# A hybrid decoder trunk: the state space branch with features on partitions

## The chip, the cores and the metric

One core of a Trainium2 chip runs the whole program. The metric is the device time of one execution in microseconds (us); the time of a kernel is the median of its runs, and a profiled execution of each kernel gives the rows shown here.

## What is computed

Two decoder layers over 512 tokens of width 1024, batch 1, all in float32. Each layer projects the normalised input once, feeds three branches (a Mamba-2 state space branch, multi-head latent attention, a gated DeltaNet), projects each branch back to the model width, merges them with gates, and adds a feed-forward part. The change lies in the state space branch. Per group g (two groups, eight heads of 64 features each) and per chunk of 128 tokens:

```python
y_diag = jnp.einsum('bclgn,bcsgn->bcgls', Cc, Bc) * L ...   # decay matrix L, per head
y_off  = jnp.einsum('bclgn,bcgepn,bgecl->bclgep', Cc, h_prev, jnp.exp(A_cum))
...
y = y + d_skip.astype(jnp.float32).reshape(G, E)[:, :, None] * xs
y = y.reshape(Bsz, S, SSD_INNER) * jax.nn.silu(z.astype(jnp.float32))
y = rmsnorm(y.reshape(Bsz, S, G, SSD_INNER // G), norm_g.reshape(G, SSD_INNER // G))
```

(The first line is shortened: the diagonal part multiplies the masked score matrix of a chunk, `CB * L`, with the head's `X = xs * dt`.) The norm runs over the 512 features of a group, for each token.

## The kernel before

**Dense products.** Every weight product is done in three parts (`mm3`, L182 to L184): the operands are split into a rounded part and a remainder, and TensorE multiplies high by high, low by high and high by low. Weights come as 512 KB tiles `wraw` through SyncE's DMA queue (`weights_raw`, L161, two buffers), ScalarE rounds them into `whi` (L154), VectorE forms the remainder `wlo` (L155), four buffers of each. `dense_F` puts features on partitions and streams the 512 tokens; `dense_T` puts tokens on partitions and streams 512 features. The activations are also kept as such pairs: `split_act` (L250, L251) and `split_gain` (L254, L255) make them.

**Order.** The engines run their lists in order. The lists are made at build time by a scheduler that keeps to data dependencies and to buffers of a tile pool (a tag has a number of buffers, and a new tile waits until the old one of that buffer has had its last reader), and that otherwise follows the program's order with some priorities. All loads and stores go through SyncE's one queue (SP), in its order. PSUM has four banks `acc` for dense products, three `sm` and one `yt` for the rest.

**The state space branch** (`ssd_group`, called for g = 0 and 1 in each layer). B and C of the group come with features on partitions (`bt`, `ctl`). The group's 512 features of x come from `dense_F` as well, go through the convolution (`conv_silu`), and are transposed on TensorE (L720) into `xs`, tokens on partitions, by ScalarE's copy (L721). z comes from `dense_T` (`silu_T`), tokens on partitions. Then a loop over the four chunks t:

- the decay matrix of eight heads (two tiles `eE` of four): a broadcast load from `d_c` in DRAM (L448), ScalarE's L450 and L451; B and C's product (L733), masked on VectorE (L735) and multiplied into `eE` (L737);
- `xd = xs * dt` (L739), the eight products of y (L742; stationary side the 128x128 decayed scores, moving side 64 features), the skip term (L744) and its addition to PSUM (L745);
- for t > 0 the contribution of the state (L748; one product, 512 columns moving), scaled by the decay (L750, a factor per row) and added (L751);
- for t < 3 the new state (L754, L756, L759 to L762);
- the gate (L764) and ScalarE's square with a running sum per row (L766).

After the loop the norm's factors come from `rsq` (L258 on VectorE, then a power on GpSimd, L259), scale the rows (L770), and sixteen transposes per block (L775) bring y to features on partitions, where `split_gain` makes the pair `yh`, `yl`. These carry the same tile names as the attention branch's output, so all but the first wait until its last products have read that.

**Around it.** Program order in a layer: front, attention branch, group 0, `gdn_decays` (decay tiles of the later branch, through `eE`, written to `d_e`, L800), half of the attention's output projection, group 1, the other half, `gdn_matrix`, `gdn_blocks` (a chain of 31 steps on VectorE, L857 and L858, and a way through DRAM), then the state space branch's output projection and the two units of the DeltaNet. The DeltaNet's triangular inverse has nine further steps of small products (`first`, L891; `second`, L907 and L908; `last_doubling`, L927 and L929). They are put between the rows of dense products:

```python
        def between():
            if next(rows) >= 23 and steps:
                steps.pop(0)()

        out_proj(a["w_ssd_out"][ly], 0, *ys, br, after=between)
```

`after` is called once per pair of weight tiles, 12 dense products; the output projection has 32 such calls.

Of the kernel before, what the change touches and what calls it, by code (L numbers as in the profile page):

```python
# [20 lines left out]
P = 128  # L21
S = 512
# [12 lines left out]
ROWS = ('ssd_dt_bias', 'gdn_dt_bias', 'ssd_a_log', 'gdn_a_log', 'ssd_d')  # L35
# [20 lines left out]
def hybrid_kernel(ctx, tc, a, out, depth=2, taps=None):  # L56
# [42 lines left out]
    ct = mk(cst, [P, NBLK * P + 104], F32, "ct")  # L99
# [195 lines left out]
    def load_params(ly, rows=True):  # L295
        pc = mk(sp, [P, 155], F32, "pc", 2)
        sync.dma_start(pc, a["pcols"][ly])
        prow = mk(sp, [P, 64], F32, "prow", 2)
        if rows:
            load_rows(prow, ly)  # L300
        return pc, prow
# [49 lines left out]
    for ly in range(depth):  # L351
# [5 lines left out]
        sconv_b, g_n1, g_ssd, g_q, g_kv, g_gdn, g_n2 = 0, 12, 20, 28, 32, 34, 35  # L357
# [32 lines left out]
        d_c = mk(dr, [T, 24 * P], F32, "d_c", 2)  # L390

        def step_sizes():
# [35 lines left out]
            sync.dma_start(d_c.rearrange("t (n l) -> (t n) l", l=P), rows)  # L428
            dec = mk(sp, [P, 3, T, 24], F32, "dec")
# [8 lines left out]
            dsk = mk(sp, [P, 16], F32, "dsk")  # L438
            dve.tensor_scalar(dsk, prow[:, 48:64], 0.25, None, ALU.mult)
# [257 lines left out]
        def ssd_group(g, yh, yl):  # L697
            h0 = 8 * g
            xs = mk(br, [P, T, 512], F32, "tok", 4)
            z = mk(br, [P, T, 512], F32, "tok", 4)  # L700
# [13 lines left out]
            for cp in range(2):  # L714
                for j, pj in enumerate(dense_F(weights(w_in, O_XBC + 512 * g + 256 * cp, 256, D), tiles(256), D, xh, xl)):
                    xf = mk(br, [P, S], F32, "ft4", 2)
                    conv(pj, 4 * g + 2 * cp + j, xf)
                    ps = sm_bank()
                    for t in range(T):
                        pe.transpose(ps[:, t * P : (t + 1) * P], xf[:, t * P : (t + 1) * P], ident)  # L720
# [4 lines left out]
            ss = mk(sp, [P, T], F32, "sss")  # L725
            st = None
            for t in range(T):
# [10 lines left out]
                xd = mk(br, [P, 512], F32, "wk0")  # L738
                dve.tensor_tensor(hv8(xd), hv8(xs[:, t, :]), bc_last(dtq[:, t, h0 : h0 + 8], 64), ALU.mult)  # L739
                py = sm_bank()  # L740
                for h in range(8):
                    pe.matmul(py[:, h * 64 : (h + 1) * 64], e2[h // 4][:, h % 4, :], xd[:, h * 64 : (h + 1) * 64], start=True, stop=True)  # L742
                y = mk(br, [P, 512], F32, "wk1")
                dve.tensor_tensor(hv8(y), hv8(xs[:, t, :]), bc_last(dsk[:, h0 : h0 + 8], 64), ALU.mult)  # L744
# [559 lines left out]
```

## Time and profile before

| | |
|---|---|
| median of 3 runs | 2329.44 us (2326.19 to 2331.61) |
| the profiled execution | 2331.74 us, of which its span 2329.9 us |
| mean granted TensorE clock | 0.993 |
| instructions in the span | 32047 |
| DMA moved | 239.85 MB, mean 103 GB/s |

The span runs from the first to the last instruction of the program; the rest of the execution's time lies around it. In a row of the order of time stand start, duration, engine, line, operation, output<-inputs, shapes and count; in brackets the idle time before it and what ended it. An ordinary float product leaves two records, one for each pass. The durations of TensorE's products overlap.

### The profile page before, as it was taken

To read this page: it belongs to the slowest core of one execution; us is meant where nothing else is said; L and a number is where in the kernel's file an instruction comes from. 1 tells how busy PE (TensorE), PEld (TensorE's weight loads), DVE (VectorE), ACT (ScalarE), POOL (GpSimd) and SP (SyncE) were. 2 spreads that over 40 slices of the span, in tenths; PEclk is the share of its full clock that TensorE was granted. 3 is DMA by queue.
4 is the path that set the end of the run, shared out by engine and by line. 5 is a ranking of instruction groups with operands and counts; after the bars stand their busy time and mean duration, and the time that the engine had idled before them with its cause. 6 is when DMAs were issued, how large, how long until landed. Compare 5 with 4: busy or idle time off the path is not lost.

```text
span 2329.9 us, 32047 instructions
## 1 busy us (share of the span) xinstructions
PE 2295.1 (99%) x11814; PEld 1891.3 (81%) x11814; DVE 1586.6 (68%) x3116; ACT 1177.7 (51%) x2455; POOL 59.2 (3%) x74
## 2 busy tenths in 40 slices
PE   9999999999999999999999999999999999999998
PEld 8888788878887888888888887888788878888886
DVE  7776666775665458767867765668656645677668
ACT  6766744333443345554657666443334434545545
POOL 0000000000000000000000000000000000000000
PEclk9999999999999999999999999999999999999999
DMA  4223533442222443233132236334422224333231
GB/s 141 78 73 91 172 100 109 123 131 82 78 78 72 145 145 109 75 116 118 50 98 78 78 94 178 91 102 143 111 84 84 67 82 154 127 118 100 91 109 46
DMA packets 208702, 239.85 MB, mean 103 GB/s; under 512 B 33888, under 2 KB 157472, under 8 KB 208544
## 3 DMA queue, kind: packets, MB, share of 16 engines
q1 hardware_dynamic: 208544, 237.80, 33.5%
q8 instruction: 93, 1.52, 0.3%
q14 instruction: 65, 0.53, 0.1%
HBM read 221.41 MB, written 11.63 MB: 100 GB/s over the span
## 4 chain that ended last, share of the span: by engine, by line
PE 89%; DVE 6%; DMA 2%; ACT 2%; POOL 1%; issue 1%; SPq 0%; DVEq 0%; POOLq 0%; ACTq 0%
PE acc L182 23%; PE acc L183 23%; PE acc L184 23%; PE sm L184 2%; PE sm L183 2%; PE sm L182 2%; DVE wlo L155 1%; PE sm L742 1%; DVE tok L858 1%; PE sm L645 1%; DVE gQ L857 1%; PE sm L1015 1%; POOL gms L259 1%; ACT whi L154 1%; PE yt L661 1%
## 5 line engine op out<-in xcount | busy, mean ns | idle before, releaser
L155 DVE TENSOR_TENSOR wlo<-wraw,whi 128x512 fp32r<-128x512 f32 (+1 forms) x552 | 377.4, 687 | 420.3 <-ACT whi L154 402.5
L154 ACT CAST whi<-wraw 128x512 fp32r<-128x512 f32 (+1 forms) x552 | 340.4, 618 | 592.7 <-PE acc L183 379.6
L184 PE MATMUL acc<-xh,wlo 128*128 128x512 f32 (+1 forms) x1248 | 487.3, 391 | 0.0
L182 PE MATMUL acc<-xh,whi 128*128 128x512 f32 (+1 forms) x1248 | 487.2, 391 | 0.0
L183 PE MATMUL acc<-xl,whi 128*128 128x512 f32 (+1 forms) x1248 | 486.3, 390 | 0.0
L183 PEld LDWEIGHTS acc<-xl,whi 128*128 128x128 f32 x1248 | 236.4, 189 | 44.3 <-DVE xl L255 0.4
L184 PEld LDWEIGHTS acc<-xh,wlo 128*128 128x128 f32 x1248 | 236.2, 189 | 44.5
L182 PEld LDWEIGHTS acc<-xh,whi 128*128 128x128 f32 x1248 | 235.9, 189 | 44.3 <-ACT xh L254 0.4
L182 PE MATMUL acc<-yh,whi 128*128 128x512 f32 x384 | 151.9, 399 | 0.0
L183 PE MATMUL acc<-yl,whi 128*128 128x512 f32 x384 | 151.3, 394 | 0.0
L184 PE MATMUL acc<-yh,wlo 128*128 128x512 f32 x384 | 151.3, 394 | 0.0
L686 DVE SCALAR_TENSOR_TENSOR ckl<-acc,pc,ckl 128x511 f32<-128x511 f32 (+2 forms) x168 | 120.3, 744 | 15.5 <-ACT ckl L682 8.2
L154 ACT CAST whi<-wr 128x512 fp32r<-128x512 f32 x128 | 79.5, 621 | 66.6 <-PE acc L184 25.9
L183 PE MATMUL acc<-wlo,xh 128*128 128x512 f32 (+1 forms) x288 | 111.2, 386 | 0.0
L184 PE MATMUL acc<-whi,xl 128*128 128x512 f32 (+1 forms) x288 | 111.0, 387 | 0.0
L182 PE MATMUL acc<-whi,xh 128*128 128x512 f32 (+1 forms) x288 | 109.6, 384 | 0.0
L182 PE MATMUL acc<-whi,yh 128*128 128x512 f32 x256 | 99.7, 389 | 0.0
L184 PE MATMUL acc<-whi,yl 128*128 128x512 f32 x256 | 99.7, 389 | 0.0
L183 PE MATMUL acc<-wlo,yh 128*128 128x512 f32 x256 | 99.6, 389 | 0.0
L155 DVE TENSOR_TENSOR wlo<-wr,whi 128x512 fp32r<-128x512 f32 x128 | 86.1, 687 | 12.1 <-ACT whi L154 11.4
L182 PEld LDWEIGHTS acc<-yh,whi 128*128 128x128 f32 x384 | 71.7, 188 | 16.7 <-ACT yh L254 1.7
L183 PEld LDWEIGHTS acc<-yl,whi 128*128 128x128 f32 x384 | 72.2, 188 | 15.2 <-issue 1.0
(418 smaller groups left out, 4532.1 us busy)
## 6 DMA issues: line engine op xcount, KB each, us to landing
wraw<-in_w_in_dram SPq DMA_DIRECT2D x144, 512.0 KB, 3.6
wraw<-in_w_up_dram SPq DMA_DIRECT2D x64, 512.0 KB, 3.6
wr<-in_w_down_dram SPq DMA_DIRECT2D x32, 1024.0 KB, 5.1
eE<-d_c SPq DMA_DIRECT2D x48, 256.0 KB, 4.0
wraw<-in_w_mla_out_dram SPq DMA_DIRECT2D x16, 512.0 KB, 3.3
eE<-d_e SPq DMA_DIRECT2D x32, 256.0 KB, 3.1
wraw<-in_w_ssd_out_dram SPq DMA_DIRECT2D x16, 512.0 KB, 3.4
wraw<-in_w_gdn_out_dram SPq DMA_DIRECT2D x16, 512.0 KB, 3.3
```

What stands on the lines that cost most here:

```text
L154: act.copy(hi, raw)
L155: dve.tensor_tensor(lo, raw, f32(hi), ALU.subtract)
L182: pe.matmul(o, ah, bh, start=start, stop=False, skip_group_check=more)
L183: pe.matmul(o, ah, bl, start=False, stop=False, skip_group_check=more)
L184: pe.matmul(o, al, bh, start=False, stop=stop, skip_group_check=more)
L259: pool.tensor_tensor(o, o, (exp if exp is not None else nhalf)[:, : o.shape[1]], ALU.pow)
L645: pe.transpose(ps[:, n : n + P], pn[t][:, kb * P : (kb + 1) * P], ident)
L661: pe.matmul(o, v_h, th[:, c : c + w], start=kb == 0, stop=False)
L686: dve.scalar_tensor_tensor(acc[:, d:], ps[:, : S - d], taps_[3 - d], acc[:, d:], ALU.mult, ALU.add)
L742: pe.matmul(py[:, h * 64 : (h + 1) * 64], e2[h // 4][:, h % 4, :], xd[:, h * 64 : (h + 1) * 64], start=True, stop=True)
L857: dve.tensor_tensor(pd, bc_last(nb[:, m, m + 1 :], m + 1), bc_mid(xb[:, m, : m + 1], 31 - m), ALU.mult)
L858: dve.tensor_tensor(xb[:, m + 1 :, : m + 1], xb[:, m + 1 :, : m + 1], pd, ALU.add)
```

## The change

In the state space branch y, z and the norm stand with features on partitions throughout.

- x is kept as it comes (`xf`, features on partitions) and scaled by the skip factor, a column of `pc` now, on ScalarE; VectorE multiplies the transposed x by dt straight out of PSUM (`xd`, for all chunks at once).
- z comes from `dense_F`.
- The products of y change operands: the stationary side is `xd` (64 columns), the moving side the 128 columns of the decayed scores. Even heads write PSUM partitions 0 to 63, odd heads 64 to 127.
- The state's contribution is four products with the state as stationary side; its decay is a factor per token, which stands along the free axis now. A new copy of the exponential of the cumulated decay is written to DRAM (`d_p`) and loaded as broadcast tiles `eb`, two DMAs per chunk.
- The norm's sum of squares: ScalarE squares, VectorE adds four feature tiles to one (two instructions), a product with a column of ones sums over the partitions (in the bank `yt`). The factors are transposed (one product per block), copied, written to DRAM (`d_r`) and loaded again as a broadcast tile `rb`, the same row for all partitions.
- y is multiplied by gain and `rb` in one VectorE instruction per feature tile and split; L775's transposes are gone. The pairs are allocated one by one.
- The tag `tok` has five buffers instead of four.
- The inverse's steps start at the 24th call of `between`, and the last of them falls into the first rows of the DeltaNet's first unit.

The core of the diff:

```diff
+            prows = mk(ml, [96, P], F32, "crowe")
+            act.activation(prows, pc_[:96, :P], AF.Exp)
+            sync.dma_start(d_p.rearrange("t (n l) -> (t n) l", l=P), prows)
...
-                    act.copy(xs[:, :, (2 * cp + j) * P : (2 * cp + j + 1) * P], ps.rearrange("p (t n) -> p t n", t=T))
-            silu_T(br, O_SZ + 512 * g, z)
+                    dve.tensor_tensor(th(xd[:, :, c * P : (c + 1) * P]), th(ps.rearrange("p (t n) -> p t n", t=T)),
+                                      bc_last(dtq[:, :, h0 + 2 * c : h0 + 2 * c + 2], 64), ALU.mult)
+                    act.activation(xf[:, c, :], xf[:, c, :], AF.Copy, scale=dsk[:, 4 * g + c : 4 * g + c + 1])
+            for cp in range(2):
+                for j, pj in enumerate(dense_F(weights(w_in, O_SZ + 512 * g + 256 * cp, 256, D), tiles(256), D, xh, xl)):
+                    silu2(z[:, 2 * cp + j, :], pj)
...
+            pss = y_bank()
...
-                xd = mk(br, [P, 512], F32, "wk0")
-                dve.tensor_tensor(hv8(xd), hv8(xs[:, t, :]), bc_last(dtq[:, t, h0 : h0 + 8], 64), ALU.mult)
                 py = sm_bank()
-                for h in range(8):
-                    pe.matmul(py[:, h * 64 : (h + 1) * 64], e2[h // 4][:, h % 4, :], xd[:, h * 64 : (h + 1) * 64], start=True, stop=True)
-                y = mk(br, [P, 512], F32, "wk1")
-                dve.tensor_tensor(hv8(y), hv8(xs[:, t, :]), bc_last(dsk[:, h0 : h0 + 8], 64), ALU.mult)
-                dve.tensor_tensor(y, y, py, ALU.add)
+                for c in range(4):
+                    for i in range(2):
+                        h = 2 * c + i
+                        pe.matmul(py[64 * i : 64 * i + 64, c * P : (c + 1) * P], xd[:, t, h * 64 : (h + 1) * 64], e2[h // 4][:, h % 4, :], start=True, stop=True)
+                y = xf[:, :, tok]
+                dve.tensor_tensor(y, y, c4(py), ALU.add)
                 if t > 0:
+                    eb = mk(br, [P, 4, P], F32, f"wk{t % 2}")
+                    for i in range(2):
+                        sync.dma_start(eb[64 * i : 64 * i + 64], d_p.rearrange("t (n l) -> t n l", l=P)[t, h0 + i : h0 + 8 : 2].partition_broadcast(64))
                     po = sm_bank()
-                    pe.matmul(po, ctl[:, tok], st, start=True, stop=True)
-                    y2 = mk(br, [P, 512], F32, "wk2")
-                    dve.tensor_tensor(hv8(y2), hv8(po), bc_last(dec[:, 0, t, h0 : h0 + 8], 64), ALU.mult)
-                    dve.tensor_tensor(y, y, y2, ALU.add)
+                    for c in range(4):
+                        pe.matmul(po[:, c * P : (c + 1) * P], st[:, c * P : (c + 1) * P], ctl[:, tok], start=True, stop=True)
+                    dve.tensor_tensor(eb, c4(po), eb, ALU.mult)
+                    dve.tensor_tensor(y, y, eb, ALU.add)
...
-                dve.tensor_tensor(z[:, t, :], z[:, t, :], y, ALU.mult)
-                jk = mk(br, [P, 512], F32, "wk2")
-                act.activation(jk, z[:, t, :], AF.Square, accum_out=ss[:, t : t + 1])
+                zt = z[:, :, tok]
+                dve.tensor_tensor(zt, zt, y, ALU.mult)
+                sq = mk(br, [P, 4, P], F32, "wk2")
+                act.activation(sq, zt, AF.Square)
+                dve.tensor_tensor(sq[:, 0:2], sq[:, 0:2], sq[:, 2:4], ALU.add)
+                dve.tensor_tensor(sq[:, 0], sq[:, 0], sq[:, 1], ALU.add)
+                pe.matmul(pss[:, t : t + 1], sq[:, 0], ones[:, 0:1], start=True, stop=True)
             rs = mk(sp, [P, T], F32, "srs")
-            rsq(rs, ss, 1.0 / 512, EPS)
-            for t in range(T):
-                dve.tensor_scalar(z[:, t, :], z[:, t, :], rs[:, t : t + 1], None, ALU.mult)
+            rsq(rs, pss[:, :T], 1.0 / 512, EPS)
+            ps = sm_bank()
+            pe.transpose(ps[:T, :P], rs, ident)
+            rsT = mk(br, [T, P], F32, "gk", 2)
+            act.copy(rsT, ps[:T, :P])
+            sync.dma_start(d_r[g].rearrange("(t p) -> t p", p=P), rsT)
+            rb = mk(br, [P, S], F32, "ft4", 2)
+            sync.dma_start(rb, d_r[g].partition_broadcast(P))
             for c in range(4):
                 k = 4 * g + c
-                ps = y_bank()
-                for t in range(T):
-                    pe.transpose(ps[:, t * P : (t + 1) * P], z[:, t, c * P : (c + 1) * P], ident)
-                split_gain(yh[k], yl[k], ps, col(g_ssd + k))
+                yn = mk(lp, [P, S], F32, f"yl{k + 1}") if k < KD - 1 else z[:, c, :]
+                dve.scalar_tensor_tensor(yn, z[:, c, :], col(g_ssd + k), rb, ALU.mult, ALU.mult)
+                yh.append(mk(lp, [P, S], F32R, f"yh{k}"))
+                yl.append(mk(lp, [P, S], F32R, f"yl{k}"))
+                split_act(yh[k], yl[k], yn)
...
-            qT = key_tiles(2 * u)
+            qT = key_tiles(2 * u, between)
...
-            if next(rows) >= 23 and steps:
+            if next(rows) >= 24 and steps:
```

More of the change, by code (lines that the diff above doesn't have):

```diff
@@ L389, in hybrid_kernel @@
         cum = mk(sp, [P, T, 24], F32, "cum")
-        d_c = mk(dr, [T, 24 * P], F32, "d_c", 2)
+        d_c, d_p = (mk(dr, [T, 24 * P], F32, n, 2) for n in ("d_c", "d_p"))
+        d_r = mk(dr, [2, S], F32, "d_r", 2)
         def step_sizes():
@@ L698, in ssd_group @@
             h0 = 8 * g
-            xs = mk(br, [P, T, 512], F32, "tok", 4)
-            z = mk(br, [P, T, 512], F32, "tok", 4)
+            xf, xd, z = (mk(br, [P, T, 512], F32, "tok", 5) for _ in range(3))
             bt, ctl = (mk(br, [P, S], F32, "ft", 6) if g else mk(lp, [P, S], F32, f"ckh{i}") for i in range(2))
@@ L844, in gdn_blocks @@
         def gdn_blocks():
[L849 removed]
+            wk = mk(br, [P, 2, 32, 32], F32, "tok", 5)
             nb, xb = wk[:, 0], wk[:, 1]
```

43 lines of the change are left out of this document (22 added, 21 removed).

## The prediction

> **What bounds the kernel now.** I read the page first, its first part and its chain.
>
> ```profile
> PE 2295.1 (99%) x11814; PEld 1891.3 (81%) x11814; DVE 1586.6 (68%) x3116; ACT 1177.7 (51%) x2455; POOL 59.2 (3%) x74
> ...
> PE 89%; DVE 6%; DMA 2%; ACT 2%; POOL 1%; issue 1%; SPq 0%; DVEq 0%; POOLq 0%; ACTq 0%
> ```
>
> TensorE is busy for 2295.1 of 2329.9 us and carries 89% of the chain; 35 us are left in which it stands. So the change is worth what it takes from or gives to TensorE's own list, plus what it does to those 35 us. A saving on VectorE or ScalarE counts only where TensorE waits for them. I therefore read next who ends TensorE's waits.
>
> ```profile
> PE sm L891 <- DMA wk<-d_x: 3.2, 2, 1.9
> ...
> PE sm L742 <- DVE eE L737: 2.3, 3, 1.3
> PE sm L487 <- DVE yh L482: 2.3, 2, 1.2
> ...
> PE yt L775 <- DVE tok L770: 1.1, 2, 0.6
> ```
>
> (Waiter, releaser, us in total, times, longest.) The state space branch owns L742 and L775, 3.4 us together; the inverse's first step owns L891, 3.2 us. Then the prices of TensorE's instructions, from the order of time in one round of the branch's loop:
>
> ```profile
> 238.61 0.40 PE L184 MATMUL acc<-xh,wlo 128*128 128x512 f32 x1
> ...
> 241.37 0.39 PE L184 MATMUL acc<-xh,wlo 128*128 128x512 f32 x1
> 241.60 1.89 PE L742 MATMUL sm<-wk,eE 128*128 128x64 f32 x16
> 243.33 1.08 PE L748 MATMUL sm<-st,ckh 128*128 128x512 f32 x2
> 244.38 1.12 PE L756 MATMUL sm<-wk,kt 128*128 128x512 f32 x2
> ```
>
> Starts are what count, since ends overlap. Twelve dense products lie between 238.61 and 241.37, so one costs 0.23 us. A product with ordinary float operands stands as two records: the 8 products of L742 are 16 passes and take 1.73 us, 0.108 each; the one product of L748 takes 1.05.
>
> **The change, part by part.** I compared the built order of both programs on each engine. The number and order of dense products is the same (8736); what differs on TensorE lies in the four state space blocks (two groups, two layers) and in the inverse.
>
> *Transposes removed.* The gated output no longer goes through the 16 transposes per block of L775, 64 in all.
>
> ```profile
> 399.11 0.60 PE L775 MATMUL yt<-ct,tok 128*128 128x128 f32 x4
> ...
> 401.40 0.60 PE L775 MATMUL yt<-ct,tok 128*128 128x128 f32 x4
> ```
>
> Four transposes and eight dense products fill 2.29 us; less 8 x 0.23 the four cost 0.45. Sixteen fours: -7.2 us.
>
> *The products of y (L742).* Operands change places: the stationary side is now 64 columns wide and the moving side 128 long, and heads alternate between the two column halves of the array. There are still 256 passes. A pass of 128 columns costs, by L1015,
>
> ```profile
> 615.72 1.05 PE L1015 MATMUL sm<-wk,eE 128*128 128x128 f32 x8
> 616.61 1.03 PE L1020 MATMUL sm<-st,ft 128*128 128x256 f32 x4
> ```
>
> 0.89 / 8 = 0.111 us, as much as the 64-column pass today. Taken one after another the 256 passes would thus stay where they are (27.7 us, 16 rounds of 1.73). But do two halves of the array run at the same time? No 128x64 product is in this trace. The nearest are the inverse's, where L907 and L908 read the same 32 rows and write different columns:
>
> ```profile
> 516.03 0.24 PE L907 MATMUL sm<-wk,ft 32*32 32x32 f32 x2
> 516.04 0.24 PE L908 MATMUL sm<-ft,wk 32*32 32x32 f32 x1
> 516.09 0.24 PE L907 MATMUL sm<-wk,ft 32*32 32x32 f32 x2
> ```
>
> Three passes start within about 0.01 us, and the next three 0.05 later. Array parts do work side by side. Against this stands the change of shape:
>
> ```profile
> 523.78 0.39 PE L184 MATMUL acc<-xh,wlo 128*128 128x512 f32 x1
> 524.10 1.14 PE L927 MATMUL sm<-tok,tok 64*64 64x64 f32 x16
> 525.17 0.50 PE L182 MATMUL acc<-yh,whi 128*128 128x512 f32 x1
> ```
>
> Entering takes 0.32 instead of 0.23 after a dense product. I take these 0.09 us for each way, in and out. In the built order the 8 products of a round are cut up by others: 1 piece in the first round, then 3, 2 and 3, or 9 per block and 36 in all: 36 x 0.18 = +6.5 us. Side by side, the pieces (8; 1, 3, 4; 4, 4; 4, 1, 3 heads) need 4.0 us per block if pairs start together, 4.6 if each product's second pass overlaps the next one's first: 16.2 to 18.4 in all. With the changes of shape 22.7 to 24.9 against 27.7: -5.0 to -2.8, I take -4. Not side by side it is 28.4 + 6.5, +7.2.
>
> [...]
>
> *The state's contribution (L748).* One product of two 512-column passes becomes four of two 128-column ones, 8 x 0.111 = 0.89 against 1.05, in 12 rounds: -1.5 us after the parting of two of them. The state update (L756) and L733 stay.
>
> *The sum of squares.* It moves from ScalarE's accumulator to TensorE: 4 products of one column per block, 32 passes in all.
>
> ```profile
> L947 PE MATMUL sm<-ct,ft 128*128 128x1 f32 x64 | 7.5, 242 | 0.0
> ```
>
> 7.5 / 64 = 0.117: +3.7 us; with four transposes of the factors (0.12 each) +4.2. I count +4.
>
> *The chain of the norm, a new wait.* After the last sum come VectorE's scale, GpSimd's power and TensorE's transpose of the factors, with only three dense products (0.68 us) ordered between the last sum and the transpose. The same chain today:
>
> ```profile
> 267.54 0.17 DVE L258 TENSOR_SCALAR srs<-sss 128x4 f32<-128x4 f32 x1
> ...
> 267.79 1.01 POOL L259 TENSOR_TENSOR srs<-srs,nhalf 128x4 f32<-128x4 f32 x1 [200.60 <-DVE srs L258]
> ...
> 268.83 0.88 DVE L770 TENSOR_SCALAR tok<-tok,srs 128x512 f32<-128x512 f32 x2 [0.54 <-POOL srs L259]
> ```
>
> 1.29 us from L258 to whoever follows, and before it the product's own 0.24 and a hand-over: about 1.65 from the sum's start, where TensorE arrives 0.8 after it. I take 0.85 us of standing, four times: +3.4. The bounds are 0 (the sum is early) and 1.2, as long as TensorE stands at L487 behind the same two instructions. What queues behind it on TensorE is the dense stream, so this is paid in full; the waits at L775 (1.1 us) go.
>
> *The loop's other work.* VectorE loses two passes over 128x512 per round and gains two short additions, and the copy from PSUM becomes its multiplication.
>
> ```profile
> 232.40:265.00 32.60, 32.05 (x165) 24.78 (x164) 27.01 (x47) 20.55 (x52) 0.00 (x0) 1.00 0.45 134
> 1385.90:1419.60 33.70, 31.93 (x165) 24.89 (x164) 27.15 (x48) 20.54 (x52) 0.00 (x0) 1.00 0.46 130
> 348.50:380.30 31.80, 31.80 (x166) 25.10 (x165) 27.46 (x48) 15.64 (x38) 0.00 (x0) 1.00 0.38 110
> ```
>
> (Window, us, busy us of TensorE, its weight loads, VectorE, ScalarE.) VectorE is at 27 of 32 us in these loops, and TensorE stands for 0.6 and 1.8 us in the first group's, 0 in the second's. The new loop asks VectorE for some 2 us less (28.2 against 30.6 us of instructions from the order, by the rows below) and is about 1 us shorter on TensorE, so it stays as tight.
>
> ```profile
> L737 DVE TENSOR_TENSOR eE<-eE,gk 128x512 f32<-128x512 f32 x8 | 5.1, 684 | 0.0
> ...
> L735 DVE SCALAR_TENSOR_TENSOR gk<-sm,ct 128x128 f32<-128x128 f32 x4 | 1.1, 284 | 0.0
> ```
>
> I followed the second group's last two rounds by hand, with some 0.6 us from one VectorE start to the next (8 of L737 cover 5.1 us), and came to waits of 0 to 0.3 us. I leave the loop's waits as they are. The 34 added DMAs all go to SP's queue. Those of the decay rows wait for a buffer freed one round earlier; the factors' round trip through DRAM, which sits between weight loads, holds the queue for the chain above and one landing, some 5 us.
>
> ```profile
> eE<-d_c SPq DMA_DIRECT2D x48, 256.0 KB, 4.0
> ```
>
> Behind it wait weight loads, needed about 70 dense products (16 us) later, and the decay tiles for the later branch. Cover enough: 0. The factors themselves are wanted only when the attention branch's tiles of the same names are free: the first block's power stands at 267.79, its next transposes at 399.11. The splits that replace L255 add 3.6 us to VectorE there, where it has this room:
>
> ```profile
> 398.00:425.00 27.00, 27.00 (x134) 22.25 (x133) 16.80 (x25) 12.07 (x20) 0.00 (x0) 1.00 0.33 93
> ```
>
> 10.2 us free of 27: 0. If that cover were gone, at most the 3.6 us per layer.
>
> *The inverse.* The first step keeps its place (1747 dense products ahead of it in both orders); the second comes one, the third nine and the rest twelve products later. So the wait at L891 stays: its data come from a chain on VectorE whose order has not changed.
>
> ```profile
> 505.49 0.39 PE L182 MATMUL acc<-xh,whi 128*128 128x512 f32 x1
> 507.75 0.44 PE L891 MATMUL sm<-wk,tok 32*32 32x32 f32 x16 [1.87 <-DMA wk<-d_x]
> ```
> ```profile
> 509.20:519.40 10.20, 10.20 (x175) 7.87 (x174) 4.45 (x8) 6.32 (x11) 0.00 (x0) 0.50 0.63 146
> 1662.90:1673.10 10.20, 10.20 (x182) 7.87 (x175) 4.45 (x8) 6.66 (x12) 0.00 (x0) 0.50 0.68 154
> ```
>
> After it the granted clock is 0.50 for 10.2 us, in each layer.
>
> ```profile
> 517.34 0.63 PE L184 MATMUL acc<-xh,wlo 128*128 128x512 f32 x1
> 517.76 0.63 PE L182 MATMUL acc<-xh,whi 128*128 128x512 f32 x1
> ```
>
> A dense product takes 0.42 us then. More of them now fall into that stretch (some 16 for 11, 0.2 us more each) and fewer small ones: +0.5 per layer, +1.
>
> **Sum.** -7.2 - 4 - 1.5 + 4 + 3.4 - 1.1 + 1 = -5.4 us. The profiled execution took 2331.74 us (span 2329.9), 2.3 over the median of 2329.44; the difference carries over: 2324.0. Its own range, from the bounds above, is 2317 to 2329.
>
> **Rivals.** *The column halves take turns.* Then y's products cost 7.2 more instead of 4 less: +5.8, 2335.2. For it: no 128-row product with half the columns is in the trace, and all 128 rows must feed two streams. Against it: L907 beside L908. It decides from a pitch of 0.088 us per pass, where the sum is zero. Chance 0.15.
>
> *The loop's waits grow.* Everything in it now passes from VectorE to ScalarE and back before TensorE's sum, and TensorE takes its list in order. If each of the 12 later rounds stood for 1.3 us, as the worst at L742 does, that is +15 to the sum: 2339. It turns the sign from 0.45 us per round. For it: VectorE at 27 of 32 us. Against it: VectorE has less to do. Chance 0.17.
>
> *The change does not move what it says, or the clock lets go.* The half clock costs up to 5.1 us per layer. In layer two TensorE stood only 1.29 us ahead of it. If the shorter program, or a late first step, brings no half clock, -4 each and part of the 3.2 us go as well: 2313 to 2317. [...] Chance 0.14.
>
> **Numbers.** Forecast 0.54, rivals 0.15, 0.17, 0.14. About 0.2% (4.7 us) is what a measurement can tell from no change. Forecast: 0.36 faster, 0.16 same, 0.02 slower; halves in turn: 0.05 same, 0.10 slower; waits: 0.02 and 0.15; clock: 0.14 faster. Together 0.50, 0.23, 0.27. The range runs from the clock's case, 2313, to near the waits' case, 2338.
>
> **What would show it.** Right: TensorE's records without L775's 64; y's products with about 0.06 us per pass; a wait of 0.85 us behind GpSimd four times; L891's wait and two half-clock stretches still there. Wrong: 0.11 us per pass, waits of over 0.5 us in each round, or a granted clock of 1.00 after L891.

## The result, and the profile after

The changed kernel took 2319.65 us (median of 5 runs, 2317.38 to 2321.44) against 2326.81 of the kernel before (2325.74 to 2331.61) on the same chip: ratio 0.9964, 95% interval 0.9950 to 0.9979, 7.2 us faster. The profiled executions differ by more, 2320.83 us (span 2319.1) and 2331.74 (span 2329.9); the last section but one of the experiments shows why.

Below, the line numbers of the changed kernel are its own: the products of y are L751 (L742 before), the state's contribution L760 (L748), the state update L767, the sums of squares L781, the factors' transpose L785, the inverse's first step L912 (L891). First the busy times and the engines' shares of the chain, from its page.

```profile
PE 2283.2 (98%) x11858; PEld 1877.5 (81%) x11858; DVE 1590.1 (69%) x3132; ACT 1177.4 (51%) x2445; POOL 59.0 (3%) x74
...
PE 89%; DVE 6%; ACT 1%; DMA 1%; POOL 1%; issue 1%; SPq 0%; DVEq 0%; POOLq 0%; ACTq 0%
```

TensorE lost 11.9 us of busy time though it has 44 records more, and it still carries 89% of the chain. So the difference lies on TensorE's own list. The stretches of that list say where. In the next two fences each row is a window (us), its length, then busy us (records) of TensorE, its weight loads, VectorE, ScalarE and GpSimd, TensorE's granted clock, the share of the DMA engines and GB/s. The windows run from one dense product to another, the same ones in both kernels: the first two rows are the state space stage of layers one and two (dense products 720 to 1370 of the layer), the last two the stage of the inverse (1740 to 1900). The kernel before:

```profile
232.36:415.38 183.02, 181.88 (x871) 146.55 (x870) 116.50 (x191) 96.99 (x211) 2.02 (x2) 1.00 0.42 124
1385.90:1570.02 184.12, 181.81 (x872) 146.62 (x871) 116.47 (x190) 97.01 (x211) 2.02 (x2) 1.00 0.43 123
504.13:558.64 54.51, 52.64 (x610) 41.95 (x609) 23.96 (x38) 22.90 (x39) 0.00 (x0) 0.91 0.37 91
1658.76:1712.69 53.93, 52.63 (x610) 41.99 (x608) 23.96 (x38) 22.91 (x39) 0.00 (x0) 0.91 0.37 92
```

The changed kernel:

```profile
230.94:411.10 180.16, 178.78 (x893) 142.33 (x892) 116.08 (x196) 96.15 (x205) 2.02 (x2) 1.00 0.46 135
1381.35:1562.26 180.91, 178.87 (x894) 142.32 (x892) 116.01 (x195) 96.03 (x205) 2.02 (x2) 1.00 0.45 134
499.84:552.99 53.15, 51.27 (x609) 40.92 (x608) 24.04 (x38) 22.89 (x39) 0.00 (x0) 0.94 0.38 95
1651.01:1701.92 50.91, 49.73 (x610) 39.74 (x608) 24.05 (x38) 22.81 (x39) 0.00 (x0) 0.97 0.39 97
```

The state space stage takes 361.07 us for 367.14: -6.1, and all of it is TensorE's busy time (357.65 for 363.69); the time in which TensorE stands there is the same, 3.4 us. The inverse takes 104.06 for 108.44: -4.4, and there the granted clock differs (0.94 and 0.97 for 0.91). Together -10.5 of the -10.9 between the two executions. The 7.2 us of the medians are less because other executions of the kernel before have less of the half clock than the profiled one: beside the experiments below, 72 of its runs (on four chips) took 2326.6 us on average at a mean granted clock of 0.9963, and the five of the changed kernel 2319.6 at 0.9964, 7.0 us less at the same clock.

What TensorE waits for, from the list of waits (us, times, longest):

```profile
PE sm L912 <- DMA wk<-d_x: 3.1, 2, 1.9
...
PE sm L785 <- POOL srs L259: 2.3, 4, 0.6
...
PE sm L751 <- DVE eE L746: 0.8, 1, 0.8
...
PE sm L751 <- ACT whi L154: 0.2, 1, 0.2
```

L775's 1.1 us are gone, the waits for the decay tiles fell from 2.3 to 1.0, and the new wait behind GpSimd is 2.3: in the branch they cancel. Last, the order of time around the new products (start, us, what): the first block's first round, then a round of the second block.

```profile
233.66 1.09 PE L751 MATMUL sm<-eE,tok 128*64 128x128 f32 x16
234.68 1.13 PE L767 MATMUL sm<-wk,kt 128*128 128x512 f32 x2
...
353.42 0.40 PE L184 MATMUL acc<-xh,wlo 128*128 128x512 f32 x1
353.80 0.40 PE L751 MATMUL sm<-eE,tok 128*64 128x128 f32 x2
354.13 0.38 PE L781 MATMUL yt<-ct,wk 128*128 128x1 f32 x2
354.44 0.65 PE L751 MATMUL sm<-eE,tok 128*64 128x128 f32 x6
355.02 0.71 PE L760 MATMUL sm<-ft,st 128*128 128x128 f32 x4
355.67 0.66 PE L751 MATMUL sm<-eE,tok 128*64 128x128 f32 x8
356.25 0.71 PE L760 MATMUL sm<-ft,st 128*128 128x128 f32 x4
356.80 0.59 PE L767 MATMUL sm<-wk,kt 128*128 128x512 f32 x1
```

Sixteen passes in one piece take 1.02 us by their starts, 0.064 each: halves at work side by side. Eight in a piece take 0.58, not 0.51, and two take 0.33; four passes of L760 behind such a piece take 0.65 (another piece follows) and 0.55 for 4 x 0.111 = 0.45. Six passes take 0.58 as well (354.44 to 355.02): of their three heads one is left without a partner in the other half. This is the price of the pieces, by which I mean runs of y's products that stand together in TensorE's list.

### The profile page after: what moved, and what is told of

It reads as the page before. It is cut to its first block, busy times and chain, and to the rows that moved or that the text cites. A ratio compares the mean times of both kernels' runs of the same rounds, so it can differ in the third digit from the quotient of the medians.

```text
span 2319.1 us, 32185 instructions
## 1 busy us (share of the span) xinstructions
PE 2283.2 (98%) x11858; PEld 1877.5 (81%) x11858; DVE 1590.1 (69%) x3132; ACT 1177.4 (51%) x2445; POOL 59.0 (3%) x74
## 3 DMA queue, kind: packets, MB, share of 16 engines
q8 instruction: 93, 1.52, 0.3%
## 4 chain that ended last, share of the span: by engine, by line
PE 89%; DVE 6%; ACT 1%; DMA 1%; POOL 1%; issue 1%; SPq 0%; DVEq 0%; POOLq 0%; ACTq 0%
PE acc L182 23%; PE acc L183 23%; PE acc L184 23%; PE sm L182 2%; PE sm L183 2%; PE sm L184 2%; DVE wlo L155 1%; PE sm L751 1%; DVE tok L879 1%; PE sm L649 1%; DVE gQ L878 1%; PE sm L1036 1%; POOL gms L259 1%; ACT whi L154 1%; PE sm L760 1%
## 5 line engine op out<-in xcount | busy, mean ns | idle before, releaser
L155 DVE TENSOR_TENSOR wlo<-wraw,whi 128x512 fp32r<-128x512 f32 (+1 forms) x552 | 377.3, 687 | 406.0 <-ACT whi L154 399.1
L184 PE MATMUL acc<-xh,wlo 128*128 128x512 f32 (+1 forms) x1376 | 536.4, 390 | 0.0
L182 PE MATMUL acc<-xh,whi 128*128 128x512 f32 (+1 forms) x1376 | 535.7, 390 | 0.0
L183 PE MATMUL acc<-xl,whi 128*128 128x512 f32 (+1 forms) x1376 | 534.9, 389 | 0.0
L184 PEld LDWEIGHTS acc<-xh,wlo 128*128 128x128 f32 x1376 | 259.6, 189 | 49.4
L183 PEld LDWEIGHTS acc<-xl,whi 128*128 128x128 f32 x1376 | 259.6, 189 | 49.1 <-DVE xl L255 0.4
L182 PEld LDWEIGHTS acc<-xh,whi 128*128 128x128 f32 x1376 | 259.1, 189 | 49.4 <-ACT xh L254 0.4
L155 DVE TENSOR_TENSOR wlo<-wr,whi 128x512 fp32r<-128x512 f32 x128 | 86.0, 686 | 12.1 <-ACT whi L154 11.4
L184 PEld LDWEIGHTS acc<-yh,wlo 128*128 128x128 f32 x384 | 72.2, 188 | 14.5
L454 ACT ACTIVATE eE<-eE,cum 128x128 f32<-128x128 f32 x192 | 63.2, 391 | 23.4 <-DMA eE<-d_c 23.4
L1236 DVE TENSOR_TENSOR h<-h,acc 128x512 f32<-128x512 f32 x96 | 61.6, 681 | 0.0
```

The lines of the kernel that those rows point to most:

```text
L155: dve.tensor_tensor(lo, raw, f32(hi), ALU.subtract)
L182: pe.matmul(o, ah, bh, start=start, stop=False, skip_group_check=more)
L183: pe.matmul(o, ah, bl, start=False, stop=False, skip_group_check=more)
L184: pe.matmul(o, al, bh, start=False, stop=stop, skip_group_check=more)
L454: act.activation(o[:, i], o[:, i], AF.Relu, scale=-1.0, bias=cum[:, t, h0 + i : h0 + i + 1])
L1236: dve.tensor_tensor(hs_, hs_, ps[t], op)
```

## The experiments

Each experiment changes the changed kernel, except where it says otherwise. Times are medians of runs beside the kernel before on the same chip; the ratio is to that one.

### The price of the transposes

```diff
             for c in range(4):
+                px = y_bank()
+                for t in range(T):
+                    pe.transpose(px[:, t * P : (t + 1) * P], z[:, c, t * P : (t + 1) * P], ident)
+            for c in range(4):
...
```

> The changed kernel with 16 idle transposes per block put back (of the gated output, into a PSUM bank that nobody reads): the price of the removed transposes by itself. The prediction's term, 64 x 0.11 = 7.2 us: 2326.9. From the stage in which they stood (16.96 us before, 13.60 after, in each of two layers): 6.7 us for 56 of them, 7.7 for 64. If they were hidden behind weight loads or waits: under 2 us.

Measured: 2324.78 us, ratio 0.9991 (0.9978 to 1.0003). That is 5.1 us over the changed kernel. The state space stage, its windows as above:

```profile
230.44:414.31 183.87, 182.68 (x926) 145.58 (x924) 115.86 (x196) 96.33 (x205) 2.01 (x2) 1.00 0.45 132
1381.34:1565.61 184.27, 182.72 (x925) 145.58 (x924) 116.00 (x195) 96.09 (x205) 2.02 (x2) 1.00 0.44 132
```

368.14 us for 361.07: 7.1 us for 64 transposes, 0.110 each, all of it busy time of TensorE (365.40 for 357.65, less 0.7 of standing). None of it was hidden. The median shows 2.0 less than the stage. This kernel's runs had a granted clock of 0.9972 on average and the changed kernel's 0.9964, which by the price found under the half clock below (1.8 us for one thousandth) is an estimated 1.4 of it.

### Do the column halves work side by side?

Two runs. The first takes a round's heads from the last decay tile to the first and keeps the halves alternating; the second takes all four heads of one half first.

```diff
-                for c in range(4):
+                for c in reversed(range(4)):
                     for i in range(2):
```
```diff
-                for c in range(4):
-                    for i in range(2):
+                for i in range(2):
+                    for c in reversed(range(4)):
```

> The changed kernel with one loop turned: the heads of a round are taken from the last decay tile to the first, so that the products of y come in about half as many pieces between full-width products (some 4 or 5 per block instead of 9). It computes the same. Theory A, each change of shape costs 0.2 to 0.3 us for a piece (the last pass of a piece 0.20 and the next product's first 0.21, where 0.11 is usual): 16 to 20 pieces fewer, -3 to -6 us, 2314 to 2317. Theory B, the price is the prediction's 0.18: -3 to -3.6. Theory C, the pieces cost nothing of their own and the times beside them are VectorE's: no change, or slower where a head's tile is awaited longer, 2319 to 2322.

> As the run with fewer pieces, but the four heads of the first column half are all taken ahead of the four of the second, so that neighbouring products write the same half of the array. It computes the same. If it is the alternation that lets two products run side by side (16 passes in 1.02 us as against 16 x 0.111 = 1.78): +0.76 for each of 16 rounds, +12 us on the run with fewer pieces, some 2328, and 16 passes of a round at about 0.11 each. If a product of 64 columns is short by itself (0.064 a pass, whatever its neighbour): no difference to the run with fewer pieces.

Measured: 2315.82 us (ratio 0.9950, 0.9938 to 0.9962) with the halves alternating, 2322.87 (0.9984, 0.9974 to 0.9994) with them in turn: 7.05 us, less than the 12 expected. The stage, alternating first, then in turn:

```profile
230.54:409.98 179.44, 176.25 (x894) 141.35 (x892) 116.54 (x196) 96.13 (x205) 2.01 (x2) 1.00 0.44 135
1376.51:1557.08 180.57, 176.24 (x894) 141.34 (x893) 116.56 (x195) 96.08 (x205) 2.01 (x2) 1.00 0.45 134
```
```profile
229.99:413.36 183.37, 180.84 (x894) 145.34 (x893) 116.97 (x196) 95.86 (x205) 2.01 (x2) 1.00 0.43 132
1380.86:1564.33 183.47, 180.84 (x894) 145.36 (x892) 117.04 (x195) 95.94 (x205) 2.01 (x2) 1.00 0.44 132
```

366.84 against 360.01 us, with 9.2 more of busy time and 2.4 less of standing. The order of time shows the same round in both, alternating:

```profile
355.25 1.09 PE L751 MATMUL sm<-eE,tok 128*64 128x128 f32 x16
356.28 1.16 PE L760 MATMUL sm<-ft,st 128*128 128x128 f32 x8
```

and in turn:

```profile
356.91 1.58 PE L751 MATMUL sm<-eE,tok 128*64 128x128 f32 x16
358.43 1.16 PE L760 MATMUL sm<-ft,st 128*128 128x128 f32 x8
```

1.03 us against 1.52 for the same 16 passes. So it is the neighbour that writes the other half which makes the passes short, not the 64 columns. In the second order some passes still overlap, where the last heads of one half meet the first of the other: in this round the eight middle passes start 0.05 to 0.06 us apart, the others mostly 0.11. That is why 16 passes take 1.52 and not 1.78, and why the loss is 0.5 a round and not 0.76. With the halves in turn this version wins 4 us on the kernel before instead of 11.

The first of these runs also prices the pieces. It has 5 pieces of y's products per block instead of 9 and fewer cuts in L760; TensorE's busy time in the stage falls from 357.65 to 352.49, 5.2 us for 16 pieces, 0.32 each, the cuts in L760 included. But the order makes TensorE stand longer, as its list of waits shows:

```profile
PE sm L785 <- POOL srs L259: 3.2, 4, 0.8
PE sm L751 <- DVE eE L746: 3.1, 4, 1.1
```

Taking the last tile first means waiting for it (3.1 us for 1.0), and the sums then end later before the norm (3.2 for 2.3). Of the 5.2 us, 1.1 are left in the stage.

### The sums of squares out of the pieces

```diff
+            sums = mk(br, [P, T, P], F32, "ft4", 2)
...
-                dve.tensor_tensor(sq[:, 0], sq[:, 0], sq[:, 1], ALU.add)
-                pe.matmul(pss[:, t : t + 1], sq[:, 0], ones[:, 0:1], start=True, stop=True)
+                dve.tensor_tensor(sums[:, t], sq[:, 0], sq[:, 1], ALU.add)
+            for t in range(T):
+                pe.matmul(pss[:, t : t + 1], sums[:, t], ones[:, 0:1], start=True, stop=True)
```

> The changed kernel with the sums of squares alone kept in one tile, so that no sum's product stands between two products of y: 7 pieces of y per block for 9, and 4 of the sums' products (two passes each) at 0.21 us for 0.31. By the traces (0.25 us for a piece, 0.10 for a sum between): 2 x 0.25 + 2 x 0.10 = 0.7 us per block, -2.8 us in all, 2316.9. If a piece costs only the 0.18 of the prediction and the sums nothing: -1.4, 2318.2. Rival: the last sum comes no later, so the stand behind GpSimd's power grows by what is saved ahead of it, 0.3 four times: -1.6.

Measured: 2313.48 us, ratio 0.9951 (0.9936 to 0.9967). The stage:

```profile
230.18:408.72 178.54, 177.13 (x893) 140.96 (x892) 115.87 (x196) 96.00 (x205) 2.01 (x2) 1.00 0.46 136
1375.19:1553.61 178.42, 177.23 (x894) 141.01 (x892) 115.89 (x195) 96.03 (x205) 2.02 (x2) 1.00 0.45 136
```

356.96 us for 361.07: -4.1, of which 3.3 busy time (354.36 for 357.65) and 0.8 waits: none of L751's is left in the list. It is more than the 2.8 expected, and the rival did not come: the wait behind the power, now L787, hardly moved.

```profile
PE sm L787 <- POOL srs L259: 2.4, 4, 0.6
```

A sum's product of two short passes was thus paid mostly through what it cut in two: 3.3 us are 0.41 for each of the eight that had stood inside a piece.

### The norm's tail later

The transpose of the factors, their trip through DRAM, the scaling and the splits are put into a function that is called after one more part of the attention branch's output projection.

```diff
-        out_proj(a["w_mla_out"][ly], 1, *y_mla, br, (0, 1))
-        ssd_group(1, *ys)
-        out_proj(a["w_mla_out"][ly], 1, *y_mla, br, (2, 3))
+        out_proj(a["w_mla_out"][ly], 1, *y_mla, br, (0,))
+        fin()
+        out_proj(a["w_mla_out"][ly], 1, *y_mla, br, (1,))
+        fin = ssd_group(1, *ys)
+        out_proj(a["w_mla_out"][ly], 1, *y_mla, br, (2,))
+        fin()
+        out_proj(a["w_mla_out"][ly], 1, *y_mla, br, (3,))
```

> The changed kernel with the tail of the group's norm (transpose of the factors, their trip through DRAM, scaling and splits) issued one part of the attention's output projection later, 15 dense products after its old place. Theory A, the stands behind GpSimd's power (2.3 us in four) are TensorE's own loss: -2.3 us, 2317.3, and that wait gone from the list. Theory B, the dense products behind them would have waited elsewhere (decay tiles, PSUM banks): 0. Rival on the other side: the scaled tiles come later and the following branch waits for them, +1 or more.

Measured: 2318.03 us, ratio 0.9963 (0.9951 to 0.9975), 1.6 under the changed kernel's median and not to be told from it. The stage and its waits:

```profile
230.76:412.32 181.56, 178.68 (x893) 142.41 (x892) 115.60 (x196) 95.71 (x205) 2.01 (x2) 1.00 0.46 134
1382.50:1562.36 179.86, 178.74 (x893) 142.45 (x892) 115.74 (x195) 95.86 (x205) 2.01 (x2) 1.00 0.46 135
```
```profile
PE sm L715 <- DVE ft L263: 2.8, 2, 2.3
```

The wait behind GpSimd is gone from the list. In layer two the stage is 1.05 us shorter; in layer one it is 1.4 longer, and most of the 2.8 us at L715, the second group's first products, are new there. The order of time of ScalarE in layer one tells who is late:

```profile
284.99 1.28 ACT L454 ACTIVATE eE<-eE,cum 128x128 f32<-128x128 f32 x4 [3.12 <-DMA eE<-d_c]
...
299.77 0.62 ACT L154 CAST whi<-wraw 128x512 fp32r<-128x512 f32 x1 [3.05 <-DMA wraw<-in_w_in_dram]
300.29 0.63 ACT L262 ACTIVATE ft<-ckl 128x512 f32<-128x512 f32 x1
```

ScalarE stands 3.05 us for a weight tile, and the step that L715 needs (L262, then VectorE's L263) is queued behind that cast. The load of weights that starts at 288.43 in the changed kernel starts at 291.12 here, and the next one at 295.43 for 292.81. Both wait for a buffer that VectorE's L155 frees, L155 waits for ScalarE's casts, and these are late too (289.77 for 287.07). What is ahead of them on ScalarE are the decay tiles of the later branch (L454): from 262 to 300 us ScalarE stands 8.2 us for their loads (3.12 of them in the row above), and 3.6 in the changed kernel. The tail's two DMAs now go into SP's queue at 276.05 and 278.30, among those loads (264.67 and 267.83 in the changed kernel). They can't be the whole cause: the longest of these stands, 3.95 us, ends at 274.60, before either. What delays the decay tiles was not tried. In layer two the stand behind GpSimd was TensorE's own and the stage gained it; in layer one the move paid it out again in another place.

### The inverse's steps, and the half clock

Three runs on the steps: back to where they were; later steps alone, on the kernel before; and one more row later. (The calls of `between` are counted from 0, so 23, 24 and 25 are the 24th, 25th and 26th call. In TensorE's list the first step stands 1747 dense products after the layer's start at 23 and at 24, and 1752 at 25. In the first two expectations the clock's window is the step of 3.413 us in which its changes lie, shown below.)

```diff
-            qT = key_tiles(2 * u, between)
+            qT = key_tiles(2 * u)
...
-            if next(rows) >= 24 and steps:
+            if next(rows) >= 23 and steps:
```

> The changed kernel with the inverse's steps back where they were (first step 1747 dense products after the layer's start as in both kernels, second 1751, third 1755, then nine earlier on). Between the two kernels the stage of the inverse (dense products 1740 to 1900) became 1.35 us shorter in layer one and 3.0 in layer two, and the half clock in it went from 10.2 us to 6.8 and 3.4. Theory A, the later steps themselves shorten the half clock: putting them back gives 10.2 us of half clock in both layers and +4.4 us, 2324. Theory B, the phase of the clock's window decides and not the steps' place: the half clock need not come back, the time stays within some 3 us of the changed kernel on either side, 2317 to 2323. My prediction's own term: the step's row costs +1, so -1, 2318.6.

> The kernel before with nothing but the later steps of the inverse; the state space branch is the old one. Theory A (the later steps shorten the half clock): -4.4 us against the kernel before, 2322.4, with 6.8 and 3.4 us of half clock. Theory B (phase of the window): 10.2 us of half clock may stay in one or both layers, and the time lies between -4 and +1 of the kernel before. The prediction's term: +1, 2327.8.

```diff
-            if next(rows) >= 24 and steps:
+            if next(rows) >= 25 and steps:
```

> The changed kernel with the inverse's steps one row of dense products later still: the first at 1752 dense products instead of 1747, the others 1764, 1776, 1788. The first step stands for its data 1.9 and 1.2 us (3.1 us in two layers). Theory A, these stands and the half clock that follows them go together: with five more dense products (1.15 us) of cover the stands fall to about 0.8 us or nothing and the half clock of 6.8 and 3.4 us is shorter or gone: -3 to -7 us, 2313 to 2317. Theory B, the half clock comes from the small products of the inverse, not from the stand: only the stand goes, -2.3. Theory C: the later steps are awaited behind the inverse instead: 0 or slower.

Measured: 2321.68 us with the steps back (ratio 0.9971, 0.9960 to 0.9982), 2324.34 with the later steps alone (0.9988, 0.9979 to 0.9997), 2313.30 with one row more (0.9943, 0.9924 to 0.9962). The stage of the inverse in the three, in that order, two layers each:

```profile
500.00:554.47 54.47, 52.66 (x609) 41.94 (x608) 23.95 (x38) 22.90 (x39) 0.00 (x0) 0.91 0.38 92
1650.80:1703.77 52.97, 50.19 (x609) 39.91 (x608) 23.94 (x38) 22.78 (x39) 0.00 (x0) 0.97 0.37 93
```
```profile
501.90:554.85 52.95, 51.27 (x610) 40.92 (x608) 24.05 (x38) 22.88 (x39) 0.00 (x0) 0.94 0.37 93
1655.57:1708.35 52.78, 51.27 (x609) 40.92 (x608) 24.04 (x38) 22.82 (x39) 0.00 (x0) 0.94 0.38 95
```
```profile
502.07:551.06 48.99, 48.28 (x609) 38.75 (x608) 24.03 (x38) 22.69 (x39) 0.00 (x0) 1.00 0.41 102
1649.04:1697.31 48.27, 48.27 (x610) 38.74 (x608) 24.04 (x38) 22.70 (x39) 0.00 (x0) 1.00 0.41 102
```

With the steps one row later still, the wait for their data is 0.7 us in one layer and none in the other:

```profile
PE sm L912 <- DMA wk<-d_x: 0.7, 1, 0.7
```

There the clock stays at 1.00 and TensorE does the stage's work in 48.3 us; what the stage took beyond that in the other rows, up to 6.2 us per layer, is the stand and the half clock behind it. The median is 6.3 us under the changed kernel's (by the ratios, 0.9943 for 0.9964, 4.9), more than the 2.4 us by which the stands shrank, and the mean granted clock of its runs is 0.9983 for 0.9964. So theory A of that run holds against its theory B. The stretches themselves, windows of the changed kernel placed on them (the first and the last are the inverses of the two layers):

```profile
505.00:511.80 6.80, 6.80 (x77) 5.22 (x76) 3.77 (x7) 5.09 (x9) 0.00 (x0) 0.50 0.90 217
1215.00:1218.40 3.40, 3.40 (x10) 2.62 (x9) 2.46 (x5) 1.78 (x4) 0.95 (x1) 0.50 0.00 0
1655.30:1658.70 3.40, 3.40 (x57) 2.45 (x58) 1.71 (x3) 2.31 (x4) 0.00 (x0) 0.50 0.90 153
```

The one between them lies ahead of layer two's attention: TensorE stands 1.15 us in front of L491, does sixteen short passes over 128 rows (eight of 128 columns, eight of one), and soon after has the half clock for 3.4 us. The kernel before has such a stretch in layer one (at 65.5 us, behind a stand of 1.1 us at the same place) and not in layer two. So the half clock is not the inverse's alone, and a run's mean granted clock counts all of it.

How long a stretch is, is not fixed by the program. With the steps at the changed kernel's place the stage ran at 0.94 and 0.97 in the changed kernel, at 0.94 twice in the run with later steps alone, and at 1.00 twice in the run with fewer pieces, whose first step stood for 1.5 and 1.3 us all the same. The kernel before varies likewise: of its runs beside the experiments, those with a mean granted clock of 0.999 took 2321.2 us (mean of 10) and those with 0.994 took 2330.6 (mean of 9), 9.4 us with nothing else changed. Fitted within each kernel over all its runs, one thousandth of granted clock goes with 1.8 us.

So between the other two runs theory B holds in part: the same steps get 0 to 10.2 us of half clock. In the traces of both kernels all changes of the clock lie whole multiples of 3.413 us apart, over the whole span (in the kernel before 1, 16, 17, 146, 149, 484 and 487 of them after the first drop, in the changed kernel 2, 208, 209, 337 and 338), so in these executions the clock changed on a fixed grid in time, and where a stand falls on that grid may differ from one execution to the next. That this alone decides was not shown. All stretches in the stages of the inverse are 3.4, 6.8 or 10.2 us long, one to three steps of the grid. Ahead of them, and of the one behind L491, TensorE stood for 1.1 to 1.9 us, with short products behind the stand: the inverse's of 32 rows and 32 columns, or the sixteen that begin with L491. Yet the steps' place is not nothing. Of the profiled stages with the steps where they were, three of four ran at 0.91 (10.2 us of half clock); of those at the changed kernel's place one of sixteen did; of those one row later still none of eight had any half clock. The medians move the same way: later steps alone are 2.6 us faster than before, with an interval that excludes zero, and steps back 2.0 slower than the changed kernel, which by itself could be chance. The profile of that run also has a stand of another kind: in layer two TensorE stands 1.58 us in front of L928, a step of the inverse, and the profile shows nothing that it waits for; that layer's 3.4 us of half clock follow this stand and not the 1.1 us in front of the first step. I take the shift's worth to be 1 to 2.6 us. By what mechanism a later second step shortens the half clock after the first was not shown.

### Together

The first combination has the heads reversed, the sums gathered and the norm's tail later; the second adds the steps one row later; the third leaves the tail of the norm where it was; the fourth has the heads in the changed kernel's order.

> Three things together on the changed kernel: the heads from the last decay tile to the first (fewer pieces), the norm's tail later, and the sums of squares kept in one tile so that their four products stand together after the loop (32 passes, 16 of them pieces of their own before, now 4 pieces). If the prices add: -3 to -6 for the pieces, -2.3 for the stands, -1 to -3 for the sums' own changes of shape: 2309 to 2314. If VectorE then bounds the loop, waits at the products of y take some of it back: 2314 to 2319.

> Everything that helped so far, together: fewer pieces, the sums gathered, the norm's tail later (2310.0 us together) and the inverse's steps one more row later (6.3 us of the changed kernel's median, of which the stand took 2.4). If the two add: 2304 to 2308, with the wait of the inverse's first step under 1 us. If the half clock, which the run with the first three seldom showed, was already most of the second gain: 2307.5, the stand's 2.4 alone.

> The best version without the later tail of the norm. If that tail's place is worth the stand in front of the factors' transpose (2.3 to 3.2 us in the runs that have it): 2.3 to 3.2 over the best version, and that wait back in the list. If it only moves the wait to the group's next products, as the run with the norm later alone showed (2.8 us in two at the first products of the second group): within 1 us of the best version.

> The best version (2306.7 us) with the heads in the changed kernel's order: 7 pieces of y per block instead of 4, but no product of y that waits for a decay tile (2.9 us in four in the best version, none in the run with the sums gathered alone). By pieces alone: 12 more at 0.25 to 0.34, +3 to +4 us, 2310 to 2311. By waits alone: -2.9, 2303.8. If the two cancel, as they did between the runs with the sums gathered (357.0 us in the state space stage) and with fewer pieces as well (357.7): 2306 to 2307.

Measured: 2310.03 us (ratio 0.9930, 0.9913 to 0.9948), 2306.70 (0.9921, 0.9906 to 0.9936), 2309.59 (0.9940, 0.9925 to 0.9956) and 2307.85 (0.9915, 0.9900 to 0.9931). The second is the best version by its median, 18.6 us under the kernel before and 13 under the changed one's median; the fourth can't be told from it. The second's waits:

```profile
PE sm L752 <- DVE eE L747: 2.9, 4, 1.1
```

The inverse's stand (L918 there) is 0.4 us. With fewer pieces there is a wait for VectorE instead: 2.9 us for decay tiles, which the heads in the changed kernel's order don't have, at the price of three more pieces per block; the two cancel, which was one of the three outcomes named. The tail's later place is worth 2.9 us by the medians here (177.2 and 177.9 us of stage for 178.9 and 178.7), where it showed next to nothing alone.

## Why the prediction was right, and where its steps were off

The forecast was -5.4 us, and the medians show -7.2. The state space branch was forecast at -6.4 (all terms but the inverse) and its stage shows -6.1; the inverse was forecast at +1 and is worth -1 to -2.6 (1.1 us are what the medians leave beside the stage; the runs on the steps gave 2.0 and 2.6). The sum came out by the right mechanism, but not with every term right.

*The transposes*: -7.2 forecast, 7.1 measured by putting 64 of them back. The step of using the cost of four transposes among dense products held to 0.1 us.

*Side by side*: right, against the rival of halves in turn, whose run lost 7 us. What was mis-sized is the change of shape. I read 0.09 us each way from a single entry of a 64-row product, and took 36 x 0.18. On the chip a piece of y's products costs about 0.32 us by the run with fewer pieces, and the order of time shows of what: 0.15 in its own passes (2 x 0.58 for 8 against 1.02 for 16), 0.10 in the first pass of what follows, and the 0.09 of entering from a dense product. That is 36 x 0.14 = 5.0 us more than I counted. On the other side a pass inside a piece costs 0.055 us (1.02 - 0.58 over 8) and not the 0.067 of my middle value (17.2 us over 256), 3 us less. The entry, all that the trace of before could show, was the smallest of the three parts.

*State's contribution and sums of squares*: no run takes either alone. By their rows each is right in its passes (0.111 us for a pass of L760), but both are cut and cut others, which the same price covers. Busy time of the stage fell by 6.0 us where my terms for TensorE made 8.7 (-7.2 - 4 - 1.5 + 4); of the missing 2.7, 2.0 are the pieces net of the cheaper passes; the rest was not taken apart.

*The norm's new wait*: four times, as forecast, 0.6 us for 0.85. The order of time shows the chain as drawn:

```profile
378.14 0.35 PE L781 MATMUL yt<-ct,wk 128*128 128x1 f32 x2
...
378.60 0.16 DVE L258 TENSOR_SCALAR srs<-yt 128x4 f32<-128x4 f32 x1
...
378.85 1.01 POOL L259 TENSOR_TENSOR srs<-srs,nhalf 128x4 f32<-128x4 f32 x1 [114.82 <-DVE srs L258]
...
379.91 0.27 PE L785 MATMUL sm<-ct,srs 128*4 128x128 f32 x1 [0.62 <-POOL srs L259]
```

From the sum to the transpose it takes 1.77 us (1.65 in the forecast); TensorE is ready 0.62 before that, 1.15 after the sum's start where I had 0.8.

*The loop's waits*: left at 2.3 in the forecast, they fell to 1.0; VectorE's busy time in the stage fell by 0.9 us (232.1 for 233.0), and whether that is why was not tried. The rival in which they grow by 15 us did not happen. With the stands at L775 gone as forecast, the waits of the branch sum to no change, where I had +2.3. I had counted on 2.7 us too much of saved busy time and on 2.3 too much waiting: they nearly cancel. That is luck, and the branch's total is better than its parts.

*The inverse*: this step was wrong. The first step kept its place and its wait (3.1 us for 3.2), as forecast, but from there I took the half clock of 10.2 us as fixed by the program, since it stood in both layers. It came to 6.8 and 3.4 us, and the other executions show that it varies from 0 to 10.2 with the steps at the same place. The rival in which the clock lets go came nearer, though it did not let go entirely (6.8 and 3.4 us were left); the step that failed is taking a length seen in one execution for a property of the program.

*The range*: the bounds written out (y's products at -5 to -2.8, the norm's stand at 0 to 1.2 us) add up to 2319.6 to 2326.6 around 2324.0. The prediction's own 2317 to 2329 is wider than they explain; the measured 2319.65 lies at the lower edge of theirs.

## What to carry to other kernels

In these runs products that write different column halves of TensorE ran side by side where they were neighbours in its list, at 0.064 us a pass for 0.11, but each further piece that full-width work made of them cost 0.32 us: put the small products that belong between them after them, and count pieces in the built order before counting passes. Where two executions of one program differ by the granted clock, compare stage by stage, with the clock column beside it, and cover a short stand ahead of small products (here 1.9 and 1.2 us, by five dense products). A wait taken away by moving work need not be gained: with the norm's tail later the stage became 1.05 us shorter in layer two and 1.4 longer in layer one.

## What the runs showed that I had not expected

After a stand of 1.1 to 1.9 us with short products behind it TensorE's granted clock was 0.50 for 3.4, 6.8 or 10.2 us, and sometimes nothing followed such a stand (1.5 and 1.3 us in the run with fewer pieces, the clock at 1.00). Covering the one ahead of the inverse took 2.4 us off the stand and in all 4.9 (by the ratios) to 6.3 us (by the medians) off the time. And a product of one column, 0.12 us per pass by itself, costs 0.31 us when it stands between two products of half width (354.13 to 354.44 above), and cuts the piece around it as well.
